# A two-layer diffusion backbone with sorted experts: the second mixer's norm by products with a diagonal, the larger experts from the fifth small one on, and the rows' gates formed ahead of the outputs

## The chip, the core and the metric

The kernel runs on one core of a Trainium2 chip. The metric is the device time of one execution in microseconds (us), in the median of several runs; less is better. A profile is one execution recorded by the hardware, and its span runs from the first instruction to the last.

The core has five engines with queues of their own, each of which works strictly in the order in which its instructions stand: TensorE (PE in the profile; PEld is its weight load), VectorE (DVE), ScalarE (ACT), GpSimd (POOL) and SyncE (SP), which here only issues transfers. An engine waits at an instruction until what it needs is there, and everything behind it in its queue waits as well.

## The reference, cut to what matters

Two layers over 512 latent tokens and 256 context tokens of width 1024, all in float32. Each layer has a mixer (attention) and a mixture of 32 experts of which each token uses two.

```python
for l in range(2):
    h_lat = modulate(x, norm_mix[l], sh1, sc1)      # rms_norm(x) * g * (1 + scale) + shift
    h_ctx = modulate(ctx, norm_mix[l], csh1, csc1)
    o_lat, o_ctx = mixer_ab(...) if l == 0 else mixer_c(...)
    x = x + gt1 * o_lat
    tokens = ...        # l == 0: context and latent tokens, 768; l == 1: latent ones, 512
    f = hier_moe(tokens, ...)                       # top 2 of 32 experts for each token
    x = x + gt2 * f                                 # l == 0: ctx = ctx + cgt2 * f[:, :c_len] too

def expert_block(xb, e):
    return (silu(xb @ w1[e]) * (xb @ w3[e])) @ w2[e]
```

An expert's output row is weighted by its token's router weight and by a gate row of 1024 numbers: gt2 for latent tokens, cgt2 for context tokens. In the second layer only latent tokens are left, so there is one gate row.

## The kernel before, in words

The program goes through setup, the first mixer with its output projection and router, the first expert stage (about 490 to 1030 us in the profile), the second mixer (mixer_c, 1030 to 1420), its output projection and router (to 1500), and the second expert stage (to the end).

*The expert stages* (moe). The experts are sorted by load while the program runs. Positions of the sorted list have a fixed room: two "static" ones and the NBIG[l] fullest ("big", 6 in the first stage and 3 in the second) hold 96 rows, the others ("small", 24 and 27) hold 64; what lies beyond goes through a loop (overflow) behind a branch, which had nothing to do in this execution. Each expert's weights come in six loads of 1 MB (line 1577) into a rotation of buffers. For each, GpSimd gathers token rows (line 1522), TensorE turns them (line 1600) and forms h = x w1 and x w3 (line 1619; 1625 for the 32 rows beyond 64 of a large expert), ScalarE and VectorE form silu and product (lines 1674, 1679), TensorE turns that (line 1688) and multiplies by w2 (tile py). VectorE then weighs py into a tile y (weigh, lines 1534 to 1538): in the first stage with sw[:, 0] times the context gate g[0] or sw[:, 1] times the latent gate g[1], one of the two weights being zero in each row, which takes three operations; in the second stage one operation is enough. GpSimd scatters y with addition into the token rows in memory (xd in the first stage, out_dram in the second, line 1528). A large expert has a second, smaller tile yt for its rows beyond 64 and so a second scatter. There are three buffers for y and one for yt.

The list `order` (lines 1540 to 1547) sets which expert is worked on when: the static ones, then the small ones with a large one behind every fourth (first stage) or ninth (second stage) of them, from the second small one on.

*What orders the instructions.* Both stages and the mixers are written as pieces (S.op) with an engine, an estimated duration, dependencies and buffer tokens (take, give). A list scheduler (Sched.run) plays these through with its own estimates before anything runs, and the order it finds is the order in which TensorE, VectorE, ScalarE and GpSimd get their instructions. SyncE's own order is made by the layer underneath.

*The second mixer's start* (mixer_c). Its six token tiles (oo[:, t]: two of context, four latent, 128 tokens each) are loaded from xd (line 1860). In memory order its buffers lie where the expert stage had its own, so its first ScalarE casts (wh, line 327) and its first loads (nw_q, nw_k, line 533) wait until the last scatter has landed. Function tokens (lines 1871 to 1881) then does for each tile: ScalarE sums the squares (line 1874), VectorE finds the reciprocal root in nine small steps (lines 289 to 301, tile css), ScalarE scales the tile in place by it, in two halves (line 1877), and flip_mod (lines 641 to 666) turns it. There TensorE transposes eight 128x128 blocks in two groups of four (line 649, tile ht), VectorE or ScalarE apply the modulation, a column scale and a shift, block by block (lines 660, 658), and the result is split into a high and a low part (chh, line 327; chl, line 330), which the projection's products (pp, lines 266 to 268) read. Context tiles are projected 256 columns wide and latent ones 384. Pieces of the projection need, beside the tiles, tables for the rotary embedding, which GpSimd forms (rope_tables, lines 528 to 548; it also issues the loads nw_q and nw_k).

Of the kernel before, what the change touches and what calls it, by code (L numbers as in the profile page):

```python
# [25 lines left out]
HD = 64  # L26
DE = 512
# [17 lines left out]
NY = 3  # L45
# [40 lines left out]
CMW = 2  # L86
# [154 lines left out]
class Backbone:  # L241
# [396 lines left out]
            self.nc.tensor.matmul(o, pts[:, b], v[b], start=b == 0, stop=b == len(v) - 1)  # L638


    def flip_mod(self, c, l, t, x, deps, tag, done, bufs, give=()):
        nc, S, v, s = self.nc, self.S, 0 if t >= NCT else 1, slice(t * 128, (t + 1) * 128)
        for g in range(2):
            cur = []

            def flip(g=g, cur=cur):
                cur.append(c.psm.tile([128, 4, 128], F32, tag="pt", name="ht"))
                for j in range(4):
                    nc.tensor.transpose(cur[0][:, j], x(4 * g + j), self.id)

            def affine(e, j, g=g, cur=cur):
                if len(cur) == 1:
                    cur.append(c.sb.tile([128, 768], F32, tag=tag, name="h", bufs=bufs)[:, 0:512]
                               .rearrange("p (j f) -> p j f", j=4))
                k = 4 * g + j
                ak, bk = self.a1[l][:, k, v:v + 1], self.mcol[l][:, k, v:v + 1]
                if e == "ACT":
                    nc.scalar.activation(cur[1][:, j], cur[0][:, j], AF.Identity, bias=bk, scale=ak)
                else:
                    nc.vector.tensor_scalar(cur[1][:, j], cur[0][:, j], ak, bk, op0=OP.mult, op1=OP.add)  # L660

            k = slice(4 * g, 4 * g + 4)
            a = S.op("PE", 0.43, flip, deps[g:g + 1] if l else deps, take=("pt", tag), give=give if g else ())
            js = [S.op(("DVE", "ACT"), (0.2, 0.25), lambda e, j=j, affine=affine: affine(e, j), [a]) for j in range(4)]
            a = S.op("-", 0.0, lambda: None, js, give=("pt",))
            done[t, g] = self.split_ops(lambda k=k, cur=cur: (c.hh[:, k, s], c.hl[:, k, s], cur[1]), 512, [a], give=(tag,))
# [823 lines left out]
    def moe(self, l, nt, oo):  # L1490
        nc, tc, i = self.nc, self.tc, self.i
        r, mm = self.rt, self.nc.tensor.matmul
        tok = nt * 128
        with ExitStack() as st:
            pool = lambda n, b, **k: st.enter_context(tc.tile_pool(name=n, bufs=b, side="right", **k))
            one = pool("moe1", 1)
            sb = pool("moesb", 2)
# [5 lines left out]
            gates, tails = [], []  # L1503
# [23 lines left out]
            def scatter(src, idx, n=DE):  # L1527
                nc.gpsimd.indirect_dma_start(out=rows(sums, n), out_offset=bass.IndirectOffsetOnAxis(ap=idx, axis=0),  # L1528
                                             in_=src, in_offset=None, bounds_check=tok * (D // n) - 1,
                                             oob_is_err=False, compute_op=OP.add)  # L1530


            def weigh(dst, src, sw, g):
                nc.vector.scalar_tensor_tensor(dst, src, sw[:, 0], g[0], op0=OP.mult, op1=OP.mult)  # L1534
                if l == 0:
                    t = sb.tile([128, DE], F32, tag="yc", name="yc", bufs=1)[:src.shape[0]]
                    nc.vector.scalar_tensor_tensor(t, src, sw[:, 1], g[1], op0=OP.mult, op1=OP.mult)
                    nc.vector.tensor_tensor(dst, dst, t, op=OP.add)  # L1538

            nb, early = NBIG[l], self.early  # L1540
            small, big = list(range(nb, NE - NST)), list(range(nb))
            order = [("static", e) for e in range(NST)]
            every = len(small) // nb
            for j, q in enumerate(small):
                order.append(("small", q))
                if j % every == 1 and big:
                    order.append(("big", big.pop(0)))
            slots = NW + self.npre + self.nmoe + NT // 2 + NEXT
            first = NW + self.npre + self.nmoe
# [2 lines left out]
            S = self.S = Sched((FPE, FDVE, FACT, FPOOL), (GPE, GDVE, GACT, GPOOL), wr=slots - len(early),  # L1552
                               xg=NX, xt=NXT, x=2, h=3, py=2, tr=3, g=2, y=NY, yt=1, u=1, v=1)
            W, X, last = {}, {}, {"mm": None, "second": None}
# [153 lines left out]
            def second(s, kind):  # L1708
                x, isb = X[s], kind != "small"
                for half in range(2):  # L1710
                    def mul(half=half):
                        if half == 0:
                            x["y"] = [pyp.tile([128, DE], F32, tag="py", name="py") for _ in range(2 if isb else 1)]
                        products(x["y"], lambda k: x["gt"][:, k, 0:CS], (lambda k: x["gt"][:, k, CS:]) if isb else None,
                                 (2 * half, 2 * half + 1), 4,
                                 lambda m, k: W[s, "w2", k // 2][0][:, 1024 * (k % 2) + 512 * m:1024 * (k % 2) + 512 * m + 512])

                    S.pos = 10.0 * s + 14.0
                    p = last["second"] = S.op("PE", 2.9 if isb else 1.9, mul, [W[s, "w2", half][1], x["gop"], last["second"]],
                                              take=() if half else ("py", "py") if isb else ("py",), give=("g",) if half else ())  # L1720
                    free(s, ("w2",), half, p)

                def out(g, token, src, gs, bufs):
                    x["o", g] = sb.tile([128, DE], F32, tag=token, name=token, bufs=bufs)[:x["parts"][g][0]]
                    weigh(x["o", g], src(), x["sw", g], gs)

                a = S.op("DVE", 0.8 if l else 2.2, lambda: out(0, "y", lambda: x["y"][0], gates, NY), [p], take=("y",), give=("py",))
                a = S.op("POOL", 1.05, lambda: scatter(x["o", 0], x["idx", 0]), [a])
                S.op("DMA", 1.1, lambda: None, [a], give=("y",))
                if isb:  # L1730
                    b, u = add_tails("py", lambda: x["y"][1], [p])
                    a = S.op("DVE", 0.8 if l else 2.2, lambda: out(1, "yt", u, tails, 1), [b], take=("yt",), give=("u",))
                    a = S.op("POOL", 1.05, lambda: scatter(x["o", 1], x["idx", 1]), [a])
                    S.op("DMA", 1.1, lambda: None, [a], give=("yt",))

# [89 lines left out]
    def mixer_c(self, oo):  # L1825
        nc, tc, i = self.nc, self.tc, self.i
        S = self.S = Sched((DPE, DDVE, DACT, DPOOL), (EPE, EDVE, EACT, EPOOL), wr=NW, pt=2, s=2, po=1, pp=1, p0=2, p1=2, pts=2, qdup=1, qhl=2, rt=1, rt1=1, hss=2, khl=1,
                           grp=2, vv=3, whl=5, mrow=2, mw=CMW)
        keep, st = ExitStack(), ExitStack()
        left = lambda n, b, **k: st.enter_context(tc.tile_pool(name=n, bufs=b, **k))  # L1830
        right = lambda n, b, **k: keep.enter_context(tc.tile_pool(name=n, bufs=b, side="right", **k))
        c = self.c = type("C", (), {})()
# [3 lines left out]
        big = left("cp", 1)  # L1836
# [21 lines left out]
        ld = S.op("DMA", 8.0, lambda: None)  # L1858

        sd = [S.op("DMA", 1.5, lambda t=t: nc.sync.dma_start(oo[:, t], self.source(1, t)), [ld]) for t in range(NT)]  # L1860
        ld = S.op("DMA", 1.0, loads, sd)
# [7 lines left out]
        hdone, spare = {}, []  # L1869

        def tokens(t):
            s = slice(t * 128, (t + 1) * 128)
            X, ss = oo[:, t], one.tile([128, 2], F32, name=f"css{t}")
            sq = S.op("ACT", 1.2, lambda: nc.scalar.activation(
                c.hh[:, :, s], X.rearrange("p (k f) -> p k f", k=KD), AF.Square, accum_out=ss[:, 0:1]), [sd[t]])
            r = self.rstd(lambda: (ss[:, 1:2], ss[:, 0:1]), D, [sq], once=t < ONCE)
            xs = [S.op("ACT", 0.6, lambda m=m: nc.scalar.activation(
                X[:, 512 * m:512 * m + 512], X[:, 512 * m:512 * m + 512], AF.Copy, scale=ss[:, 1:2]), [r]) for m in range(2)]
            self.flip_mod(c, 1, t, lambda k: X[:, 128 * k:128 * k + 128], xs, "p0", hdone, 2)
            if t >= 4:  # L1880
                spare.extend([hdone[t, 0], hdone[t, 1]])

        for t in range(NT):
            S.pos = -38.0 + t
            tokens(t)
        tables = S.op("POOL", 4.0, tables, [], pos=-24.0)


        def lam_dots():
# [3 lines left out]
        a = S.op("POOL", 0.5, lam_dots, [ld], pos=-20.0)  # L1893
        a = S.op("DVE", 0.2, lambda: nc.vector.tensor_reduce(ls, lp[:, 0::2], axis=AX.X, op=OP.add), [a], pos=-20.0)
        a = S.op("ACT", 0.1, lambda: nc.scalar.activation(ls, ls, AF.Exp), [a], pos=-20.0)
# [14 lines left out]
        room = [oo[:, 4 + m // 2, 512 * (m % 2):512 * (m % 2) + 512] for m in range(4)]  # L1910
# [169 lines left out]
```

## Time and profile before

| | us |
|---|---|
| runs | 2027.43, 2023.10, 2027.01 |
| median | 2027.01 |
| the profiled execution | 2027.06 |
| its span | 2025.2 |
| TensorE busy in the span | 1767.7 (87%) |
| VectorE busy | 1022.0 (50%) |
| ScalarE busy | 559.3 (28%) |
| GpSimd busy | 335.7 (17%) |

The views used here are these. The windows give each engine's busy time in a stretch of the span, the clock granted to TensorE (1.00 is full speed) and the mean share of time in which the 16 DMA engines were busy; this share comes out a little above 1 when they are full. The timeline lists instructions in order of time: start, duration, engine, line, operation, output<-input, count, and in brackets the idle time of the engine just before it and what ended that, as far as the semaphore events tell. The grouped lines give for each line and shape the busy time, the mean duration in ns, and the idle time before. For TensorE the duration of one instruction includes its way through the array, and neighbours overlap; start to start tells the rate. Indirect DMAs on GpSimd show the time in which it prepares them, not their landing.

### The profile page before, as it was taken

What the parts mean: (1) busy time and instruction counts of PE and PEld (TensorE: products, weight loads), DVE (VectorE), ACT (ScalarE), POOL (GpSimd) and SP (SyncE); (2) the same over time, 40 slices, a digit from 0 to 9 for tenths busy, and PEclk for the clock granted to TensorE, in tenths of its full rate; (3) what the DMA queues carried; (4) which work ended last, traced back from release to release, by engine and by line L of the source; (5) the groups of instructions that cost most, each with busy time, mean ns of one, the idle gap of its engine ahead of it and who ended that gap; (6) DMA issues with size and microseconds to landing.
All of it is one profiled execution on the core that took longest, in us unless ns stands there. A gap on an engine that the chain in (4) does not pass through costs nothing. (4 is left out here: it accounts for less than half of the span.)

```text
span 2025.2 us, 27795 instructions
## 1 busy us (share of the span) xinstructions
PE 1767.7 (87%) x10130; PEld 1013.8 (50%) x10130; DVE 1022.0 (50%) x2628; ACT 559.3 (28%) x1278; POOL 335.7 (17%) x365
## 2 busy tenths in 40 slices
PE   4999998896999898888938999998869998978986
PEld 2798776684233222222327989996752332222322
DVE  3788878597333232333357788887872211211211
ACT  4565556321110000000044555555311100000000
POOL 1001000012122112111112232221021221111111
PEclk8999999897999999999959999999879999999999
DMA  8502314337999999999933222115569999999996
GB/s 354 188 20 82 141 47 167 146 125 262 356 385 403 407 407 410 407 405 406 389 121 115 74 74 63 32 42 183 206 241 343 386 408 413 409 413 413 409 412 249
DMA packets 98782, 532.42 MB, mean 263 GB/s; under 512 B 22840, under 2 KB 23208, under 8 KB 43344
## 3 DMA queue, kind: packets, MB, share of 16 engines
q1 hardware_dynamic: 82544, 509.53, 63.4%
q0 software_dynamic: 16096, 21.05, 4.4%
q8 instruction: 82, 1.34, 0.3%
q14 instruction: 60, 0.49, 0.1%
HBM read 517.45 MB, written 29.03 MB: 270 GB/s over the span
## 5 line engine op out<-in xcount | busy, mean ns | idle before, releaser
L1619 PE MATMUL h<-wr,x 128*64 128x512 f32 x2000 | 530.3, 612 | 92.1 <-DMA wr<-in_w_dram 90.0
L1619 PEld LDWEIGHTS h<-wr,x 128*64 128x64 f32 x2000 | 149.4, 138 | 401.8 <-issue 225.4
L1605 DVE COPY x<-trx 128x512 f32<-128x512 f32 (+1 forms) x67 | 43.8, 659 | 462.3 <-PE trx L1600 462.2
L1619 PE MATMUL py<-wr,gt 128*64 128x512 f32 x1024 | 240.4, 599 | 2.3 <-DMA wr<-in_w_dram 1.7
L1674 ACT ACTIVATE sl<-h 64x512 f32<-64x512 f32 x64 | 37.8, 591 | 702.7 <-PE h L1619 696.0
L1619 PEld LDWEIGHTS py<-wr,gt 128*64 128x64 f32 x1024 | 68.5, 136 | 137.5 <-issue 121.8
L266 PE MATMUL pp<-wh,chh 128*128 128x384 f32 (+1 forms) x384 | 132.6, 345 | 4.5 <-ACT vv L692 2.7
L1679 DVE TENSOR_TENSOR gp<-sl,h 64x512 f32<-64x512 f32 x64 | 68.0, 1062 | 122.4 <-ACT sl L1674 121.8
L268 PE MATMUL pp<-wh,chl 128*128 128x384 f32 (+1 forms) x384 | 124.6, 325 | 1.1 <-DVE chl L330 1.1
L267 PE MATMUL pp<-wl,chh 128*128 128x384 f32 (+1 forms) x384 | 124.6, 325 | 0.0
L1522 POOL DMA_INDIRECT xg<-h2d,ridx x64 | 68.3, 1067 | 281.3 <-PE trx L1600 242.8
L1534 DVE SCALAR_TENSOR_TENSOR y<-py,rsw,g 128x512 f32<-128x512 f32 x64 | 48.1, 751 | 126.4 <-PE py L1619 124.7
L623 PE MATMUL ptp<-cst,p 128*128 128x128 f32 x592 | 95.4, 284 | 17.6 <-DVE p L1955 4.5
L1528 POOL DMA_INDIRECT xd<-y,ridx x32 | 53.5, 1672 | 234.2 <-DVE y L1538 146.1
L1528 POOL DMA_INDIRECT out_dram<-y,ridx x32 | 52.7, 1646 | 216.0 <-DVE y L1534 177.3
L623 PEld LDWEIGHTS ptp<-cst,p 128*128 128x128 f32 x592 | 69.0, 143 | 36.5 <-issue 15.1
L1193 POOL TENSOR_TENSOR h2p<-xi,bc 128x512 f32<-128x512 f32 x10 | 16.2, 1618 | 410.7 <-DVE xi L1190 320.8
L946 ACT ACTIVATE p<-s,nbias,r 128x256 f32<-128x256 f32 (+3 forms) x96 | 76.6, 801 | 17.9 <-DVE nbias L940 8.0
L266 PEld LDWEIGHTS pp<-wh,chh 128*128 128x128 f32 x384 | 74.7, 195 | 11.4 <-ACT vv L692 7.4
L627 ACT COPY pts<-ptp 128x384 f32<-128x384 f32 (+2 forms) x114 | 54.9, 488 | 77.9 <-PE ptp L623 77.4
L268 PEld LDWEIGHTS pp<-wh,chl 128*128 128x128 f32 x384 | 74.3, 193 | 1.4 <-DVE chl L330 1.4
L267 PEld LDWEIGHTS pp<-wl,chh 128*128 128x128 f32 x384 | 74.7, 194 | 0.0
(347 smaller groups left out, 3262.3 us busy)
## 6 DMA issues: line engine op xcount, KB each, us to landing
wr<-in_w_dram SPq DMA_DIRECT2D x378, 1024.0 KB
wr<-in_w_mod_dram SPq DMA_DIRECT2D x48, 1024.0 KB
wr<-in_wc_dram SPq DMA_DIRECT2D x16, 768.0 KB
wr<-in_wab_dram SPq DMA_DIRECT2D x8, 768.0 KB
oo<-in_w_dram SPq DMA_DIRECT2D x6, 1024.0 KB
h2d<-h2p SPq DMA_DIRECT2D x10, 512.0 KB
bc<-modrow SPq DMA_DIRECT2D x9, 512.0 KB
wr<-in_w_out_ab_dram SPq DMA_DIRECT2D x4, 1024.0 KB
```

Of the source, the lines that this page charges most:

```text
L266: mm(ps, xh, wh, start=start, stop=False)
L267: mm(ps, xh, wl, start=False, stop=False)
L268: mm(ps, xl, wh, start=False, stop=stop)
L623: nc.tensor.transpose(st[g][:, b], st["p"][:, (g + b) * 128:(g + b + 1) * 128], self.id)
L627: f(st["pts"][:, g:g + n], st[g][:, :n])
L946: nc.scalar.activation(p[:, a:b], st["s"][:, a:b], AF.Exp, bias=nb()[:, m:m + 1], scale=hr()[:, m:m + 1], accum_out=z["ssum"][:, h + m:h + ...
L1522: nc.gpsimd.indirect_dma_start(out=dst, out_offset=None, in_=rows(self.h2d[l], n), in_offset=bass.IndirectOffsetOnAxis(ap=idx, axis=0), bo ...
L1528: nc.gpsimd.indirect_dma_start(out=rows(sums, n), out_offset=bass.IndirectOffsetOnAxis(ap=idx, axis=0), in_=src, in_offset=None, bounds_ch ...
L1534: nc.vector.scalar_tensor_tensor(dst, src, sw[:, 0], g[0], op0=OP.mult, op1=OP.mult)
L1605: (nc.scalar.copy if e == "ACT" else nc.vector.tensor_copy)(x["x"][:, 512 * g:512 * g + 4 * w].rearrange("p (k t) -> p k t", k=4), x["tr", g])
L1619: mm(out[0][CS * m:CS * m + CS], at(k), w(m, k), start=k == 0, stop=k == n - 1, tile_position=(0, CS * m), skip_group_check=True)
L1679: nc.vector.tensor_tensor(x["p"][dst].rearrange("t (k p) -> t p k", k=4), v(a), v(b), op=OP.mult)
```

## The change

There are three parts, and what follows from them in the order of instructions.

1. In the second mixer, the tile is no longer scaled in place. VectorE writes a 128x128 diagonal dg, the identity times the reciprocal root of each token, and flip_mod multiplies each block by it (an ordinary product where a transpose with the identity stood), so that turning and scaling are one. The diagonals lie in two buffers that later pieces use (qdup and csq), taken in turn. The tables of the rotary embedding now depend on the loads of the token tiles having been issued (`[ld]`).

2. In the expert stages, the first large expert comes behind the fifth small one, and the others behind every third (first stage) or seventh (second stage) from there.

3. In the first stage, the tile y is filled ahead of the output with the gates: sw[:, 0] * g[0] + sw[:, 1] * g[1], two operations that need the expert's gt but not its last product; then one multiplication by py is left (out). In the second stage only the buffer is taken sooner.

```diff
-    def flip_mod(self, c, l, t, x, deps, tag, done, bufs, give=()):
+    def flip_mod(self, c, l, t, x, deps, tag, done, bufs, give=(), by=None):
...
-                    nc.tensor.transpose(cur[0][:, j], x(4 * g + j), self.id)
+                    if by is None:
+                        nc.tensor.transpose(cur[0][:, j], x(4 * g + j), self.id)
+                    else:
+                        nc.tensor.matmul(cur[0][:, j], x(4 * g + j), by(), start=True, stop=True)
...
             def weigh(dst, src, sw, g):
...
+                if l:
+                    nc.vector.scalar_tensor_tensor(dst, src, sw[:, 0], g[0], op0=OP.mult, op1=OP.mult)
+                else:
+                    row_gates(dst, sw, g)
+                    nc.vector.tensor_tensor(dst, src, dst, op=OP.mult)
+            def row_gates(dst, sw, g):
+                nc.vector.tensor_scalar(dst, g[0], sw[:, 0], None, op0=OP.mult)
+                nc.vector.scalar_tensor_tensor(dst, g[1], sw[:, 1], dst, op0=OP.mult, op1=OP.add)
...
-            every = len(small) // nb
+            every = (len(small) - 4) // nb
             for j, q in enumerate(small):
                 order.append(("small", q))
-                if j % every == 1 and big:
+                if j >= 4 and (j - 4) % every == 0 and big:
                     order.append(("big", big.pop(0)))
...
-                a = S.op("DVE", 0.8 if l else 2.2, lambda: out(0, "y", lambda: x["y"][0], gates, NY), [p], take=("y",), give=("py",))
+                a = S.op("DVE", 0.02 if l else 1.1, lambda: room(0, "y", gates, NY), [x["gop"]], take=("y",))
+                a = S.op("DVE", 0.8, lambda: out(0, lambda: x["y"][0], gates), [p, a], give=("py",))
...
-            xs = [S.op("ACT", 0.6, lambda m=m: nc.scalar.activation(
-                X[:, 512 * m:512 * m + 512], X[:, 512 * m:512 * m + 512], AF.Copy, scale=ss[:, 1:2]), [r]) for m in range(2)]
-            self.flip_mod(c, 1, t, lambda k: X[:, 128 * k:128 * k + 128], xs, "p0", hdone, 2)
+            def diagonal():
...
+                nc.vector.tensor_scalar(dg[0], self.id, ss[:, 1:2], None, op0=OP.mult)
+            r = S.op("DVE", 0.2, diagonal, [r], take=(room,))
+            self.flip_mod(c, 1, t, lambda k: X[:, 128 * k:128 * k + 128], [r, r], "p0", hdone, 2, give=(room,), by=lambda: dg[0])
...
-        tables = S.op("POOL", 4.0, tables, [], pos=-24.0)
+        tables = S.op("POOL", 4.0, tables, [ld], pos=-24.0)
```

The lines are renumbered by the change (line 1528 before is 1531 after, 1860 is 1877, 649 is 652).

GpSimd's queue at the end of the first expert stage, before: scatters of y and yt into xd, and the gathers xg that stand between them; the branch to the overflow follows.

```order
L1528 DMA xd<-y,ridx_3696 1536x512
L1522 DMA xg_5678<-h2d_89,ridx_3696 128x512
L1528 DMA xd<-y,ridx_3696 1536x512 x4
L1528 DMA xd<-yt,ridxt 1536x512
L1528 DMA xd<-y,ridx_3696 1536x512 x2
```

And the same place after the change:

```order
L1531 DMA xd<-y,ridx_3696 1536x512
L1525 DMA xg_5678<-h2d_89,ridx_3696 128x512
L1531 DMA xd<-y,ridx_3696 1536x512 x2
L1531 DMA xd<-yt,ridxt 1536x512
L1531 DMA xd<-y,ridx_3696 1536x512 x4
```

The scatter yt of the last large expert has moved from third to fifth from the end.

SyncE's queue where the second mixer begins, before: the rows' weights nw, the six tiles oo, the small vector lp, and two loads of weights (wr).

```order
L533 DMA nw_q<-in_qn_c_dram 128x64
L533 DMA nw_k<-in_kn_c_dram 128x64
L1860 DMA oo<-xd 128x1024 x6
L1852 DMA lp<-in_lam_c_dram 128x256
L1758 DMA wr<-in_wc_dram 128x1536
L381 DMA wr<-in_w_mod_dram 128x2048
```

And after the change:

```order
L1877 DMA oo<-xd 128x1024 x6
L1869 DMA lp<-in_lam_c_dram 128x256
L533 DMA nw_q<-in_qn_c_dram 128x64
L533 DMA nw_k<-in_kn_c_dram 128x64
L381 DMA wr<-in_w_mod_dram 128x2048 x2
```

The nw loads have moved behind the tiles. The last load of wc stands ahead of the branch to the overflow now, together with the three others, and a load of w_mod that stood among them has moved behind nw_k.

TensorE's queue in the second mixer, where the turning of the last tiles meets the projection of the first latent tile (products of width 384), before:

```order
L268 MATMUL pp<-wh,chl 128x256
L649 MATMUL ht<-cst,oo 128x128 x16
L266 MATMUL pp<-wh,chh 128x384
L267 MATMUL pp<-wl,chh 128x384
L268 MATMUL pp<-wh,chl 128x384
```

And after, from the fourth tile's second half on:

```order
L268 MATMUL pp<-wh,chl 128x256
L652 MATMUL ht<-dg,oo 128x128 x4
L266 MATMUL pp<-wh,chh 128x384
L267 MATMUL pp<-wl,chh 128x384
L268 MATMUL pp<-wh,chl 128x384
```

Where all sixteen blocks of the last two tiles stood ahead of the first product of width 384, only the last four of the fourth tile do now; the last two tiles' blocks follow in fours, with six to twelve products between them. On ScalarE the twelve scalings are gone from this place, and the sums of squares of the last three tiles stand together.

More of the change, by code (lines that the diff above doesn't have):

```diff
@@ L1533, in weigh @@
             def weigh(dst, src, sw, g):
[L1534 to L1538, printed above, removed]
+                if l:
[6 more added lines that the diff above has]
+                nc.vector.scalar_tensor_tensor(dst, g[1], sw[:, 1], dst, op0=OP.mult, op1=OP.add)
             nb, early = NBIG[l], self.early
@@ L1721, in second, with room, out @@
                     free(s, ("w2",), half, p)
-                def out(g, token, src, gs, bufs):
+                def room(g, token, gs, bufs):
                     x["o", g] = sb.tile([128, DE], F32, tag=token, name=token, bufs=bufs)[:x["parts"][g][0]]
-                    weigh(x["o", g], src(), x["sw", g], gs)
-                a = S.op("DVE", 0.8 if l else 2.2, lambda: out(0, "y", lambda: x["y"][0], gates, NY), [p], take=("y",), give=("py",))
+                    if l == 0:
+                        row_gates(x["o", g], x["sw", g], gs)
+                def out(g, src, gs):
+                    if l:
+                        weigh(x["o", g], src(), x["sw", g], gs)
+                    else:
+                        nc.vector.tensor_tensor(x["o", g], src(), x["o", g], op=OP.mult)
+                a = S.op("DVE", 0.02 if l else 1.1, lambda: room(0, "y", gates, NY), [x["gop"]], take=("y",))
+                a = S.op("DVE", 0.8, lambda: out(0, lambda: x["y"][0], gates), [p, a], give=("py",))
                 a = S.op("POOL", 1.05, lambda: scatter(x["o", 0], x["idx", 0]), [a])
@@ L1731, in second @@
                     b, u = add_tails("py", lambda: x["y"][1], [p])
-                    a = S.op("DVE", 0.8 if l else 2.2, lambda: out(1, "yt", u, tails, 1), [b], take=("yt",), give=("u",))
+                    a = S.op("DVE", 0.02 if l else 1.1, lambda: room(1, "yt", tails, 1), [x["gop"]], take=("yt",))
+                    a = S.op("DVE", 0.8, lambda: out(1, u, tails), [b, a], give=("u",))
                     a = S.op("POOL", 1.05, lambda: scatter(x["o", 1], x["idx", 1]), [a])
@@ L1827, in mixer_c @@
         S = self.S = Sched((DPE, DDVE, DACT, DPOOL), (EPE, EDVE, EACT, EPOOL), wr=NW, pt=2, s=2, po=1, pp=1, p0=2, p1=2, pts=2, qdup=1, qhl=2, rt=1, rt1=1, hss=2, khl=1,
-                           grp=2, vv=3, whl=5, mrow=2, mw=CMW)
+                           grp=2, vv=3, whl=5, mrow=2, mw=CMW, csq=1)
         keep, st = ExitStack(), ExitStack()
@@ L1876, in tokens @@
             r = self.rstd(lambda: (ss[:, 1:2], ss[:, 0:1]), D, [sq], once=t < ONCE)
-            xs = [S.op("ACT", 0.6, lambda m=m: nc.scalar.activation(
-                X[:, 512 * m:512 * m + 512], X[:, 512 * m:512 * m + 512], AF.Copy, scale=ss[:, 1:2]), [r]) for m in range(2)]
-            self.flip_mod(c, 1, t, lambda k: X[:, 128 * k:128 * k + 128], xs, "p0", hdone, 2)
+            dg, room = [], "qdup" if t % 2 else "csq"
+            def diagonal():
+                dg.append(c.sb.tile([128, 2, 2, HD], F32, tag="qdup", name="dg", bufs=1).rearrange("p a b d -> p (a b d)")[:, 0:128] if t % 2
+                          else c.sb.tile([128, 128], F32, tag="csq", name="dg", bufs=1))
+                nc.vector.tensor_scalar(dg[0], self.id, ss[:, 1:2], None, op0=OP.mult)
+            r = S.op("DVE", 0.2, diagonal, [r], take=(room,))
+            self.flip_mod(c, 1, t, lambda k: X[:, 128 * k:128 * k + 128], [r, r], "p0", hdone, 2, give=(room,), by=lambda: dg[0])
             if t >= 4:
```

## The prediction

> **What bounds the kernel now.** I read the windows first, to see which engine sets the pace in each stage, then TensorE's waits, then the timeline of the seam between the first expert stage and the second mixer, instruction by instruction. The windows give for each stretch the busy time (and count) of TensorE, its weight loads, VectorE, ScalarE and GpSimd, then TensorE's granted clock, the DMA share and GB/s.
>
> ```profile
> 600.00:700.00 100.00, 92.26 (x438) 29.06 (x436) 33.73 (x47) 7.52 (x14) 22.86 (x17) 1.00 1.02 404
> 1010.00:1020.00 10.00, 5.02 (x22) 1.20 (x18) 4.20 (x6) 0.00 (x0) 1.56 (x1) 0.91 0.40 138
> 1020.00:1030.00 10.00, 0.00 (x0) 0.00 (x0) 0.00 (x0) 0.00 (x0) 1.56 (x1) 0.50 0.11 16
> 1570.00:1580.00 10.00, 10.00 (x52) 3.60 (x50) 3.18 (x5) 0.59 (x1) 5.47 (x4) 1.00 0.95 344
> 1580.00:1590.00 10.00, 10.00 (x62) 2.73 (x58) 1.44 (x2) 0.37 (x1) 2.66 (x2) 1.00 0.98 376
> 1800.00:1900.00 100.00, 83.92 (x384) 26.70 (x382) 17.08 (x21) 7.48 (x15) 15.90 (x12) 1.00 1.02 413
> ```
>
> Inside both expert stages the DMA share stands at 1.02 and TensorE waits for weights, so the order of the experts can't shorten the stream itself, except where the share is below that. Between 1020 and 1030 us nothing computes at all. The timeline of that hole:
>
> ```profile
> 998.72 1.56 POOL L1528 DMA_INDIRECT xd<-y,ridx  x1 [11.69 <-DVE y L1538]
> 1008.37 1.42 POOL L1528 DMA_INDIRECT xd<-yt,ridxt  x1 [8.09 <-DVE gp L1679]
> 1009.21 1.94 PE L1619 MATMUL py<-wr,gt 128*64 128x512 f32 x8 [0.55 <-DMA wr<-in_w_dram]
> 1012.63 0.69 DVE L1538 TENSOR_TENSOR y<-y,yc 128x512 f32<-128x512 f32 x1
> 1014.18 1.94 PE L1619 MATMUL py<-wr,gt 128*64 128x512 f32 x8 [0.46 <-DMA wr<-in_w_dram]
> 1015.69 1.56 POOL L1528 DMA_INDIRECT xd<-y,ridx  x1 [5.90 <-issue]
> 1017.61 0.69 DVE L1538 TENSOR_TENSOR y<-y,yc 128x512 f32<-128x512 f32 x1
> 1023.74 1.56 POOL L1528 DMA_INDIRECT xd<-y,ridx  x1 [6.48 <-SPq L1772]
> 1030.11 0.34 SPq L533 DMA_DIRECT2D nw_q<-in_qn_c_dram  x1
> 1030.50 0.42 SPq L533 DMA_DIRECT2D nw_k<-in_kn_c_dram  x1
> 1030.51 3.03 ACT L327 CAST wh<-wr 128x768 fp32r<-128x768 f32 x4 [23.45 <-DMA xd<-y,ridx]
> 1031.05 3.51 SPq L1860 DMA_DIRECT2D oo<-xd  x6
> 1035.89 1.06 ACT L1874 ACTIVATE chh<-oo 128x1024 fp32r<-128x1024 f32 x1 [2.35 <-DMA oo<-xd]
> ```
>
> The last output is ready at 1018.30 (1017.61 + 0.69), but its scatter starts at 1023.74. The four scatters start 9.65, 7.32 and 8.05 us apart: each adds into the same tensor xd and starts only when the one ahead has landed. The reasons in the brackets (a branch, "issue") are guesses of the view; the even spacing, with the data long ready, is what I go by. The chain holds four links because the last large expert, with two scatters, stands third from the end. At 1030.11 the last one has landed, and ScalarE and the DMA queue both come free on it: that seam is what the change can move.
>
> **The change part by part.** Everything is counted against the profiled execution, 2027.06 us (its span is 2025.2), which is the median, 2027.01, to 0.05 us.
>
> *Experts in another order, first stage.* The last large one now has four small ones behind it, 24 loads of 1 MB or about 60 us of stream at 404 GB/s, so its scatters are done long before. Left of the chain are the last two small outputs. *Gates formed ahead:* behind the last product stands one VectorE operation instead of three. The one before last ends its products at 1011.15 (1009.21 + 1.94); one operation of 0.69 makes 1011.9, and the queue's step, 0.28 elsewhere at a scatter that waited for data alone (its y done at 984.65, start 984.93), 1012.2. The rows for this and for the next part, timeline first, then loads with their sizes:
>
> ```profile
> 983.96 0.69 DVE L1538 TENSOR_TENSOR y<-y,yc 128x512 f32<-128x512 f32 x1
> 984.93 2.11 POOL L1528 DMA_INDIRECT xd<-y,ridx  x1 [15.90 <-DVE y L1538]
> 2009.53 1.56 POOL L1528 DMA_INDIRECT out_dram<-y,ridx  x1 [13.00 <-DVE y L1534]
> 2014.47 1.56 POOL L1528 DMA_INDIRECT out_dram<-y,ridx  x1 [3.39 <-DVEq L1772]
> ...
> 1072.78 0.73 POOL L555 TENSOR_TENSOR qk<-qk,nw_k 128x256 f32<-128x256 f32 x1 [27.58 <-ACT sq L701]
> ...
> wr<-in_w_dram SPq DMA_DIRECT2D x378, 1024.0 KB
> oo<-xd SPq DMA_DIRECT2D x6, 512.0 KB
> ```
>
> The last scatter follows one interval later. I take 8.05, that of the same pair before, so 1020.2; its landing took 6.37 (1030.11 - 1023.74), so 1026.6: 3.5 us earlier. Bounds of the interval: 9.65, the longest of the chain above (gain 1.9), and 4.94, the pair at the end of the second stage, where little else moved (then the last output's own time decides, 1016.12 + 0.69 + 0.28 + 6.37 = 1023.5, gain 6.6). The end of the weight stream, which both rely on, I leave where it is, as the same bytes are loaded. The added gate operations lie beside other work: VectorE is busy 33.73 of 100 us there. If that cover failed, two operations of 0.7 us would stand before a product of an early expert, where TensorE is full.
>
> *SyncE's queue.* The two nw loads no longer stand ahead of the six oo loads: 0.94 us (1031.05 - 1030.11) is taken off their issue; at least 0.5, should the first issue after the wait cost more. The nw loads now land behind 3 MB of oo and GpSimd forms its tables later. The cover is long: the first operation on them is at 1072.78, after a wait of 27.58 us, and those tables were done when it began. What the queue gains in addition, the second half of the next group's weights ahead of the branch, nobody waits for.
>
> *The mixer's norm.* Twelve ScalarE scalings go, six small VectorE operations that form a diagonal come, and the eight transposes of a token become products with it.
>
> ```profile
> L1877 ACT ACTIVATE oo<-oo,css 128x512 f32<-128x512 f32 x12 | 8.3, 715 | 0.8 <-DVE css L301 0.5 <-DVE rsv L289 0.3
> L660 DVE TENSOR_SCALAR h<-ht,a,mcol 128x128 f32<-128x128 f32 x36 | 12.9, 406 | 6.6 <-ACT h L658 4.7 <-PE ht L649 1.9
> L289 DVE TENSOR_SCALAR rsv<-css 128x1 f32<-128x1 f32 x6 | 0.9, 148 | 2.1 <-ACT chh L1874 2.1
> 1307.10 0.96 PE L623 MATMUL ptp<-cst,p 128*128 128x128 f32 x6 [0.66 <-DVE p L1955]
> 1307.82 0.36 PE L266 MATMUL pp<-wh,chh 128*128 128x256 f32 x1
> 1309.31 1.50 PE L638 MATMUL po<-vv,pts 128*128 128x128 f32 x12
> 1310.65 0.60 PE L729 MATMUL ptk<-cst,khl 128*128 128x128 f32 x4
> 1036.00:1071.30 35.30, 18.40 (x97) 16.61 (x97) 25.40 (x97) 26.68 (x51) 3.95 (x10) 0.65 0.32 118
> 1040.50:1071.30 30.80, 18.40 (x97) 16.61 (x97) 22.38 (x84) 22.68 (x44) 0.69 (x2) 0.67 0.21 74
> 1059.02 1.97 PE L649 MATMUL ht<-cst,oo 128*128 128x128 f32 x8 [4.90 <-ACT oo L1877]
> 1070.53 1.11 PE L649 MATMUL ht<-cst,oo 128*128 128x128 f32 x4 [1.82 <-ACT oo L1877]
> 1071.30 0.67 PE L266 MATMUL pp<-wh,chh 128*128 128x384 f32 x1
> ```
>
> The trace has real products of this very shape: twelve (L638) take 1.34 us to the next instruction, 0.11 each, and six transposes (L623) 0.72, or 0.12 each. So I cost the products at nothing. A page speaks against that: the Trainium skill, "TensorE: Matmul & The Clock Gate", section "Terms", says that transpose mode is four times faster for FP32. Read as a price for the plain product, it gives the third rival below; these rows don't bear it out.
>
> A diagonal (128x128, from SBUF) has no row; it lies between 0.15 (one column, L289) and 0.41 (same size, from PSUM), and I take 0.3, in the middle. The first token's first scaling of 0.72 becomes that: 0.4 us. Behind it, from 1040.5 to 1071.3, TensorE is idle for 12.4 of 30.8 us, on chains through ScalarE and VectorE. 6.72 us of it (4.90 + 1.82) end on a scaling. Not all goes, since the sums of squares and the root ahead of it take their time too; but the new order also lets products of width 384 begin before the last transposes, where now all wait until 1071.30. I take two thirds, 4.5 us. The floor is 0, if the planner's new order gives it back; the ceiling is VectorE's own work: 25.40 busy of 35.30, plus 6 x 0.3, leaves 8.1. Behind this ramp the instructions stand as before, so what is gained is kept.
>
> *Second stage's order.* There the share is 0.95 and 0.98 while the first large expert fills TensorE (1570 to 1590); a small one in its place frees buffers sooner. 0.7 + 0.4 us to reach 1.02 make 1.1 at most, 0 at least; I take 0.8. In the first stage the same place shows no loss.
>
> Sum: 3.5 + 0.9 + 0.4 + 4.5 + 0.8 = 10.1, so 2027.06 - 10.1 = 2017.0. All upper ends give 6.6 + 0.9 + 0.6 + 8.1 + 1.1 = 17.3 (2009.8), all lower ends 1.9 + 0.5 + 0.3 = 2.7 (2024.4).
>
> **The rivals.** *The ramp gives nothing:* with ScalarE relieved, VectorE's in-order queue (22.38 of 30.8 us busy, now with six operations more) is late next, and TensorE waits for its splits instead. For it: 36 affine operations of 0.41 are VectorE's already. Against: ScalarE was as busy, and is what the two longest waits name. It leaves 5.6 us: 2021.5. *The chain isn't shortened:* the interval of the last pair is set by transfers still queued (the share is 0.40 until 1020), not by the scatter, and stretches to 9.65; with a ramp of nothing that is the lower end, 2024.4, within 0.2%. For it: those queued loads stay. *The product costs four times a transpose* (slower): 3 x 0.12 us at full clock, twice that at the 0.50 that the clock has behind the hole, for 48 of them is 17 to 35 us of TensorE, say 26; 12.4 idle us swallow part, the other terms give 5.2 back: 2027.06 + 26 - 12.4 - 5.2 = 2035. It decides from an extra of (12.4 + 5.2) / 48 = 0.37 us each. Against it stand the L638 rows.
>
> **How the numbers follow.** Forecast 0.62, ramp of nothing 0.20, chain not shortened 0.12, dear products 0.06. 2017.0 is the first case; the range 2009.8 to 2024.4 takes in the first three, with all bounds. No change that can be told is within 0.2%, 4.1 us, so down to 2023.0. The first case and nearly all of the second lie below that: faster 0.80; the third and what is left of the second: same 0.14; slower 0.06.
>
> **What would show it.** The seam: two scatters a chain apart at the end, the last output's behind one VectorE operation, ScalarE's idle stretch of 23.45 us cut by 3 to 4, oo issued first. The ramp: no wait on a scaling, the first product of width 384 some 5 us sooner after the first sum of squares than the 35.4 us (1071.30 - 1035.89) of now. The second stage: share 1.02 from 1570 on. Wrong it would be if the last two scatters still stand four deep, if the products take more than 0.2 us each at full clock, or if the ramp is as long as before with VectorE named.

## The result, and the profile after

The changed kernel takes 2013.12 us in the median of five runs (2011.08 to 2016.79), the kernel before 2027.01 in five beside them (2023.10 to 2030.90): the ratio is 0.9938, with a 95% interval of 0.9923 to 0.9953, or 13.9 us between the medians where 10.0 were forecast. The profiled execution took 2011.99 us with a span of 2010.2, against 2025.2: 15.0 us between the spans.

The windows after the change, with the same columns as before (the last three are TensorE's granted clock, the DMA share and GB/s):

```profile
1010.00:1020.00 10.00, 5.95 (x28) 1.84 (x24) 2.52 (x4) 0.37 (x1) 1.56 (x1) 1.00 0.42 150
1020.00:1030.00 10.00, 0.00 (x0) 0.00 (x0) 1.52 (x2) 2.38 (x4) 1.56 (x1) 0.57 0.33 100
1036.00:1071.30 35.30, 28.15 (x188) 26.83 (x188) 27.35 (x100) 22.76 (x51) 8.90 (x17) 0.92 0.17 69
```

The hole behind the stage is still there. In the ramp, the stretch that held 18.40 us of TensorE's work now holds 28.15; the ramp begins some 5 us sooner in it. The timeline of the seam after the change:

```profile
1011.72 0.69 DVE L1740 TENSOR_TENSOR y<-py,y 128x512 f32<-128x512 f32 x1 [1.76 <-PE py L1627]
1012.53 3.98 PE L1627 MATMUL py<-wr,gt 128*64 128x512 f32 x16 [0.46 <-ACT gt L1700]
1012.68 1.56 POOL L1531 DMA_INDIRECT xd<-y,ridx  x1 [13.38 <-DVE y L1740]
1016.56 0.69 DVE L1740 TENSOR_TENSOR y<-py,y 128x512 f32<-128x512 f32 x1 [2.97 <-PE py L1627]
1020.98 1.56 POOL L1531 DMA_INDIRECT xd<-y,ridx  x1 [6.73 <-DMA xd<-y,ridx]
1026.58 2.81 SPq L1877 DMA_DIRECT2D oo<-xd  x6
1030.83 0.33 SPq L533 DMA_DIRECT2D nw_q<-in_qn_c_dram  x1
1030.94 1.06 ACT L1891 ACTIVATE chh<-oo 128x1024 fp32r<-128x1024 f32 x1 [0.29 <-DMA oo<-xd]
1034.03 0.29 DVE L1900 TENSOR_SCALAR dg<-cst,css 128x128 f32<-128x128 f32 x1
1034.53 3.75 PE L652 MATMUL ht<-dg,oo 128*128 128x128 f32 x16 [18.02 <-ACT chh L1891]
```

Two scatters stand a chain apart, the last output (ready at 1017.25) behind one operation of VectorE, and oo ahead of nw. The last row is the surprise: one token's eight products are sixteen instructions.

Six distances place the gain of the profiled executions, 15.0 us in all. They run between the starts of rows as above; the first scores are the first product s<-kt, and the order of these products on TensorE is the same in both:

| us | before | after | gain |
|---|---|---|---|
| last scatter starts | 1023.74 | 1020.98 | 2.76 |
| from there to the first sum of squares | 12.15 | 9.96 | 2.19 |
| from there to the first scores | 69.04 | 62.56 | 6.48 |
| from there to the output projection's first product | 324.99 | 323.53 | 1.46 |
| from there to the loads of the second stage's gates | 70.18 | 68.68 | 1.50 |
| from there to the end | 525.1 | 524.5 | 0.6 |

The last three rows, 3.6 us, differ as much between kernels that are the same there, so they are not put down to the change; the figures stand further below.

### The profile page after: what moved, and what is told of

Same layout as the page of the kernel before. It is cut to its first block, busy times and chain, and to the rows that moved or that the text cites. A ratio compares the mean times of both kernels' runs of the same rounds, so it can differ in the third digit from the quotient of the medians.

```text
span 2010.2 us, 27841 instructions
## 1 busy us (share of the span) xinstructions
PE 1768.0 (88%) x10178; PEld 1015.5 (51%) x10178; DVE 1010.9 (50%) x2625; ACT 553.4 (28%) x1275; POOL 336.4 (17%) x365
## 5 line engine op out<-in xcount | busy, mean ns | idle before, releaser
L1613 DVE COPY x<-trx 128x512 f32<-128x512 f32 (+1 forms) x75 | 48.1, 651 | 485.9 <-PE trx L1608 485.8
L931 DVE TENSOR_REDUCE nbias<-s 128x1 f32<-128x768 f32 (+3 forms) x80 | 64.8, 814 | 19.2 <-PE s L609 16.9
```

The lines of the kernel that those rows point to most:

```text
L931: nc.vector.tensor_reduce(nb(), st["s"][:, off:off + w].rearrange("p (n f) -> p n f", n=n), axis=AX.X, op=OP.max, negate=True)
L1613: (nc.scalar.copy if e == "ACT" else nc.vector.tensor_copy)(x["x"][:, 512 * g:512 * g + 4 * w].rearrange("p (k t) -> p k t", k=4), x["tr", g])
```

## The experiments

Twelve kernels, each timed in five rounds against the kernel before. The two distances are those of the table's second and third rows; nw or oo names what stands first in SyncE's queue.

| kernel | median us | ratio to before, 95% | scatter to squares | squares to scores |
|---|---|---|---|---|
| order_only | 2022.79 | 0.9975 to 0.9993 | 13.23, nw | 68.55 |
| gates_only | 2032.56 | 1.0022 to 1.0046 | 12.81, nw | 67.48 |
| order_gates | 2024.82 | 0.9984 to 1.0004 | 12.63, nw | 67.57 |
| gates_yt2 | 2025.14 | 0.9986 to 1.0003 | 13.16, nw | 68.41 |
| tables_late_before | 2023.20 | 0.9978 to 0.9998 | 9.81, oo | 68.30 |
| norm_only | 2017.31 | 0.9944 to 0.9971 | 9.73, oo | 62.29 |
| tables_early | 2018.78 | 0.9958 to 0.9980 | 13.39, nw | 65.13 |
| transposes_back | 2011.97 | 0.9916 to 0.9943 | 10.03, oo | 60.55 |
| mask_transpose | 2015.08 | 0.9924 to 0.9950 | 9.99, oo | 60.96 |
| warm | 2014.43 | 0.9925 to 0.9948 | 10.03, oo | 62.85 |
| warm_before | 2025.47 | 0.9989 to 1.0006 | 13.85, nw | 67.80 |
| warm_stages | 2013.61 | 0.9930 to 0.9957 | 10.02, oo | 62.48 |

The theory was the prediction's three parts, with the clock as what made the ramp gain more; its rivals were that one part carries all, and that the clock is a bystander.

**The three parts alone.**

```diff
 # order_only: before, with
+            every = (len(small) - 4) // nb
+                if j >= 4 and (j - 4) % every == 0 and big:
```

> The kernel before with the new order of the experts alone, in both stages. Theory (chain of scatters): the last two scatters of the first stage are those of two small experts, the one before last waits for its output's two operations more than in the changed kernel (about 1.4 us), the last follows an interval of 8 us later; so the mixer's loads are issued about 2 us sooner than the 1031.05 of before, and the second stage gives 0.7 to 0.9: 2.0 to 4.0 us faster than before in all. Rival (the stream sets the end, the order is worth nothing): within 1 us of before. Second rival (the order alone carries the whole seam, the gates nothing): 3.5 us or more at the seam.

It gained 3.7 us (medians of 2026.53 and 2022.79), as the theory had it. Its timeline, TensorE's last products of the stage and the last three scatters:

```profile
1015.49 1.94 PE L1619 MATMUL py<-wr,gt 128*64 128x512 f32 x8 [0.25 <-DMA wr<-in_w_dram]
1000.47 1.56 POOL L1528 DMA_INDIRECT xd<-y,ridx  x1 [12.57 <-DVE y L1538]
1014.92 1.56 POOL L1528 DMA_INDIRECT xd<-y,ridx  x1 [12.89 <-DVE y L1538]
1023.47 1.56 POOL L1528 DMA_INDIRECT xd<-y,ridx  x1 [6.99 <-DMA xd<-y,ridx]
```

The last scatter starts only 0.27 us sooner than before (1023.47 against 1023.74), but this execution's whole first stage lies later: the first load of its gates is issued at 487.76 instead of 485.50, ahead of anything that the edit touches. Counted from the end of TensorE's last product (1017.43 here, 1016.12 before), the last scatter starts 6.04 us behind it instead of 7.62. So the order alone does shorten the chain, to two links and by 1.6 us. This distance is 7.0 to 7.6 in the four profiles that leave this stage as before, 6.7 and 6.5 in the two with the gates alone (gates_only, gates_yt2, below), and 4.5 to 4.9 in the seven with both. The 0.7 to 0.9 us that were expected of the second stage aren't there (525.2 us from its gates' loads to the end, against 525.1); what else makes up the 3.7 is not shown.

```diff
 # gates_only: before, with row_gates, room and out of the change
+                a = S.op("DVE", 0.02 if l else 1.1, lambda: room(0, "y", gates, NY), [x["gop"]], take=("y",))
```

> The kernel before with the rows' gates formed ahead of the outputs alone. Theory (chain of scatters): the chain of four stands, but its first link waits for an output that is ready about 1.4 us sooner, so the seam comes 0 to 1.4 us sooner and the total is within 1.5 us of before. Rival (what stands behind the last product decides, not the chain): the mixer's loads are issued 1.4 us or more sooner and the last two scatters no longer wait for each other.

Both expectations fell: it is 6 us slower than before (2032.56 against 2026.53). The timelines of VectorE and TensorE at the front of the first stage, in this kernel:

```profile
558.13 0.48 DVE L1542 TENSOR_SCALAR yt<-g2t,rswt 64x512 f32<-64x512 f32 x1 [10.92 <-DMA xd<-yt,ridxt]
559.42 1.03 DVE L1684 TENSOR_TENSOR gp<-sl,h 64x512 f32<-64x512 f32 x1
560.50 0.69 PE L1693 MATMUL trg<-cst,gp 64*128 64x64 f32 x4 [4.85 <-DVE gp L1684]
```

The gates of the next large expert's yt stand in VectorE's queue until the last scatter of yt, of which there is one buffer, has landed. Behind them stands gp, for which TensorE waits 4.85 us. In the changed kernel VectorE waits at the same kind of place:

```profile
557.82 0.48 DVE L1545 TENSOR_SCALAR yt<-g2t,rswt 64x512 f32<-64x512 f32 x1 [6.63 <-DMA xd<-yt,ridxt]
```

What stands behind it there is wanted later: TensorE's wait for gp between 520 and 620 us (in total, times, longest) comes to

```profile
PE trg L1696 <- DVE gp L1687: 0.2, 1, 0.2
```

```diff
 # norm_only: before, with the diagonal, flip_mod(by=) and
+        tables = S.op("POOL", 4.0, tables, [ld], pos=-24.0)
```

> The kernel before with the mixer's norm by products with a diagonal alone (GpSimd's tables behind the loads of the tokens with it). Theory (scalings gone, then the clock comes back sooner): TensorE's clock is at half for under 10 us between the first products of the ramp and its end, against 25 us before; the ramp is 6 to 8 us shorter, the queue gives 0.9: 8 to 11 us faster than before. Rival (the ramp's gain needs the shorter hole of the seam, by where the clock's windows fall): 3 to 6 us faster. Second rival (SyncE's queue and the scalings alone, as the prediction had it): 5.8 us.

It gained 9.2 us, the ramp 6.75 (69.04 to 62.29), within the theory's numbers. Whether the clock was the reason is tested below.

**Order and gates together, and the cause of the loss.**

```diff
 # order_gates: before, with both of the parts above
 # gates_yt2: gates_only, with
-                               xg=NX, xt=NXT, x=2, h=3, py=2, tr=3, g=2, y=NY, yt=1, u=1, v=1)
+                               xg=NX, xt=NXT, x=2, h=3, py=2, tr=3, g=2, y=NY, yt=2, u=1, v=1)
+                    a = S.op("DVE", 0.02 if l else 1.1, lambda: room(1, "yt", tails, 2), [x["gop"]], take=("yt",))
```

> The kernel before with the experts' order and the gates ahead together, the mixer as before. Theory (the two need each other: the order takes the third user of the yt buffer away from the front, the gates take two operations out of the last chain): the last scatter starts near 1021 as in the changed kernel, the front of the stage loses nothing, the rest behind the last scatter is as before; 3 to 5 us faster than before, about 2022. Rival (the parts add up: 3.7 us gained by the order alone, 6 lost by the gates alone): 2 to 3 us slower than before.

> The kernel with the gates alone, and two buffers for the output yt of the large experts instead of one. Theory (with one buffer the gates of the next large expert wait in VectorE's queue for the scatter of the last, 10.9 us, and hold up what TensorE needs): that wait is under 2 us, TensorE does not stand at the front of the stage, and the loss of 6 us is gone: 2024.5 to 2027.5. Rival (the gate operations themselves, ahead of work that TensorE waits for, cost the time): still 2030 or more.

With a second buffer the loss is gone (2025.14), and no wait for yt stands among VectorE's waits from 520 to 1020: the cause is shown. Order and gates together gain 2.0 us of medians, below the 3 to 5 expected and above the sum of the two, which would be 2.3 slower; the interval takes in both no gain and the lower end of the theory. The last scatter, at 1020.86, is where it was expected.

**SyncE's queue.**

```diff
 # tables_early: the changed kernel, with
+        tables = S.op("POOL", 4.0, tables, [], pos=-24.0)
 # tables_late_before: before, with
+        tables = S.op("POOL", 4.0, tables, [ld], pos=-24.0)
```

> The changed kernel with GpSimd's tables free of the wait for the tokens' loads, as before, so that the two loads of nw stand ahead of the six of oo in SyncE's queue again. Theory (SyncE's queue): oo is issued 0.9 us later behind the last scatter's landing, and the whole is 0.5 to 1 us slower than the changed kernel. Rival (GpSimd's tables, 9 us later in the changed kernel, cost the mixer something): 0.5 us or more faster than the changed kernel.

> The kernel before with nothing but GpSimd's tables behind the tokens' loads, so that the six loads of oo go ahead of the two of nw. Theory (SyncE's queue: in the runs so far the first sum of squares starts 12.2 to 13.9 us behind the last scatter's start with nw first, 9.7 to 10.0 with oo first): 9.7 to 10.0 us here too, the total 2 to 3.5 us faster than before, about 2024. Rival (the queue is worth 0.9 us, and what the changed kernel with the tables early lost came from its own order of work in the ramp): within 1.5 us of before.

The queue is worth more than 0.9 us. By medians, nw first costs the changed kernel 5.7 (2018.78 against 2013.12), and oo first gains the one before 3.6 (2023.20 against 2026.83; that interval by itself, 0.4 to 4.5, would allow the 0.9). The distance from scatter to squares is the clearer measure. The timeline with nw first, in tables_early:

```profile
1020.25 1.56 POOL L1531 DMA_INDIRECT xd<-y,ridx  x1 [6.74 <-DMA xd<-y,ridx]
1026.51 0.34 SPq L533 DMA_DIRECT2D nw_q<-in_qn_c_dram  x1
1026.90 0.74 SPq L533 DMA_DIRECT2D nw_k<-in_kn_c_dram  x1
1027.76 3.25 SPq L1877 DMA_DIRECT2D oo<-xd  x6
1033.64 1.06 ACT L1891 ACTIVATE chh<-oo 128x1024 fp32r<-128x1024 f32 x1 [3.70 <-DMA oo<-xd]
```

And with oo first, in tables_late_before:

```profile
1025.20 1.56 POOL L1528 DMA_INDIRECT xd<-y,ridx  x1 [6.29 <-SPq L1772]
1030.71 3.04 SPq L1860 DMA_DIRECT2D oo<-xd  x6
1035.01 1.06 ACT L1874 ACTIVATE chh<-oo 128x1024 fp32r<-128x1024 f32 x1 [0.23 <-DMA oo<-xd]
```

Three things add up. The first load is issued 6.26 us behind the scatter when it is nw, 5.51 when it is oo; the two nw take 1.25 more; and the squares of oo's first tile start 5.88 us behind its issue instead of 4.30. Why the first issue and the tile come later behind nw, no run shows. In all seven profiles with oo first the squares start 9.7 to 10.0 us behind the scatter, in the seven with nw first 12.2 to 13.9 (the 13.9 is warm_before, below, whose first issue comes only 8.07 us behind the scatter; without it, 12.2 to 13.4). The rest of the loss in tables_early is in the ramp. There the planner puts an operation of the mixer's lambda elsewhere, and the table that ScalarE loads for it with it:

```profile
1057.65 1.28 ACT L1919 ACT_TABLE_LOAD   x1
```

In the changed kernel this stands at 1059.50, 28.6 us behind the first sum of squares instead of 24.0, and among modulations too. The ramp of tables_early is 2.57 us longer (65.13 against 62.56); whether the table load's place makes any of that wasn't tried.

**The product's price.**

```diff
 # transposes_back: the changed kernel, with
+                    if True:
+                        nc.tensor.transpose(cur[0][:, j], x(4 * g + j), self.id)
 # mask_transpose: the changed kernel, with
+                        nc.tensor.transpose(cur[0][:, j], x(4 * g + j), by())
+                nc.vector.tensor_scalar(dg[0], self.id, ss[:, 1:2], 0.0, op0=OP.mult, op1=OP.is_gt)
```

> The changed kernel with the 48 products with the diagonal turned back into transposes of the unscaled tokens; the diagonal is formed and waited for as before, but the norm's scaling is left out of what is computed. Theory (a product costs about 0.2 us at full clock, a transpose 0.12): 48 x 0.08 to 0.1 is 4 to 5 us of TensorE, of which the idle time of the ramp hides about half: 1.5 to 4 us faster than the changed kernel. Rival (product and transpose cost the same, as the prediction had it): within 0.5 us of the changed kernel. Second rival (four times a transpose): 10 us or more faster.

> The changed kernel with the 48 products turned into transposes that still wait for the same operation of VectorE: it forms a matrix of zeros and ones from the same column instead of the diagonal, so every wait and every engine's order stays; the norm's scaling is left out of what is computed. Theory (a product takes about 0.2 us at full clock and 0.47 at half, a transpose 0.12 and 0.25): the first eight take 1.8 us less at half clock, ahead of everything, and the rest 0.08 each, of which waiting hides half: 2 to 4 us faster than the changed kernel, about 2010. Rival (product and transpose cost the same): within 0.5 us of the changed kernel, about 2013.

The first was badly made: an unscaled transpose needs no diagonal, so the first ones ran at 1031.67, ahead of the squares at 1032.03, and the wait was gone as well. The second keeps every wait and order. TensorE's groups of these instructions (busy us, mean ns), first in the changed kernel, then in mask_transpose:

```profile
L652 PE MATMUL ht<-dg,oo 128*128 128x128 f32 x96 | 15.0, 313 | 19.4 <-ACT chh L1891 18.0 <-DVE dg L1900 1.4
```

```profile
L652 PE MATMUL ht<-dg,oo 128*128 128x128 f32 x48 | 9.3, 338 | 19.2 <-ACT chh L1891 18.1 <-DVE dg L1900 0.7 <-ACT h L661 0.4
```

A plain product of this shape is two instructions (96 for 48 products), and the 48 cost 5.7 us more of TensorE in all, 0.12 each at the clocks that the two ramps have. The ramp was 1.6 us shorter with transposes (60.96 against 62.56); in the medians (2015.08 and 2013.12) nothing of it shows.

**The clock.**

```diff
 # warm: the changed kernel (warm_before: the one before), ahead of the mixer's pieces
+        wm = psm.tile([128, 4, 128], F32, tag="pt", name="wm")
+        for k in range(80):
+            nc.tensor.matmul(wm[:, k % 4], self.id, self.id, start=True, stop=True)
 # warm_stages: the changed kernel, 15 such products ahead of each stage's S.run()
```

> The changed kernel with 80 products of the 128x128 identity with itself on TensorE in the hole between the first expert stage and the mixer (about 16 us at full clock, from 1016.5 on; their result goes nowhere). Theory (the clock falls behind the hole and is half the ramp's cost that is left): the clock is at 1.0 when the ramp begins, the first eight products take 1.8 us instead of 3.75, the half-speed windows of the ramp go, 2 to 4 us faster than the changed kernel, about 2010. Rival (the ramp is a chain through ScalarE and VectorE, TensorE's speed in it is idle time): within 1 us of the changed kernel.

> The kernel before with the same 80 products in its hole (from 1016 on, done by about 1033 of the hole that ends at 1040.5). Theory (the clock, once it has fallen, comes back only with a nearly full window, and the waits for scalings keep it from that): the windows at half speed behind the hole, 25 us of them before, are halved at least, and the ramp is 3 to 6 us shorter than in the kernel before, about 2021 to 2024. Rival (the waits for scalings by themselves cost the time, the clock is a bystander): within 1.5 us of before, with the waits for scalings as long as before or longer.

> The changed kernel with 15 products of the identity with itself on TensorE at the front of each expert stage (about 1497.5 to 1504.5 in the second, while it waits for the first tokens). Theory (the clock is at 0.5 for 30.7 us at the front of each stage, and TensorE is full behind it for 80 us with the weights' stream below its 1.02): the clock is at 1.0 some 13 us sooner, TensorE does 5 to 7 us of work sooner in each stage, and 2 to 6 us of each are kept: 2002 to 2009. Rival (the stream of weights binds the stages anyway, as the ramp was bound by its chain when the clock was held up there): within 1.5 us of the changed kernel.

The windows of warm show how far the clock was held:

```profile
1020.00:1030.00 10.00, 10.00 (x92) 10.00 (x91) 0.97 (x2) 1.83 (x3) 1.56 (x1) 1.00 0.29 74
1030.00:1040.00 10.00, 8.34 (x75) 8.14 (x73) 6.57 (x23) 6.16 (x12) 0.00 (x0) 1.00 0.86 332
1040.00:1050.00 10.00, 7.75 (x40) 7.25 (x40) 9.01 (x33) 5.46 (x12) 6.35 (x13) 0.66 0.38 161
```

It was at 1.00 through the hole and the first token's products, and fell again behind them: 0.66 from 1040 to 1050, where the changed kernel has this:

```profile
1040.00:1050.00 10.00, 7.18 (x46) 6.78 (x46) 9.32 (x35) 5.32 (x11) 6.34 (x13) 0.83 0.35 148
```

Nothing came of it: the scores follow the squares by 62.85 us (62.56 without), although the first token's products took 1.95 us instead of 3.75. The extra products also ended late and put the first real one at 1036.39, 4.87 behind the squares instead of 3.59, which takes back 1.28 of these 1.80 us. In warm_before the distance fell by 1.2 (69.04 to 67.80) and the total is not to be told from before; there too the clock fell again, to 0.57 from 1040 to 1050.

So the gains that the theory of the clock expected, 2 to 4 and 3 to 6 us, did not come, and a full clock in the hole and at the first products is worth nothing that can be told. No run held the clock through the whole ramp, though. In the kernel before it is at 0.67 from 1050 to 1060, 0.84 to 1070 and 0.69 to 1080; in the changed one it is at 1.00 from 1050 on. How much of the ramp's gain is this return, how much the scalings' steps that are gone, and how much the new order of products, is not separated. That the steps on ScalarE and VectorE carry it is the likelier reading, not a shown one.

In warm_stages the clock returned sooner too, 0.85 against the changed kernel's 0.50 from 500 to 510:

```profile
500.00:510.00 10.00, 7.36 (x49) 5.98 (x50) 2.85 (x10) 0.00 (x0) 6.04 (x7) 0.85 1.01 409
```

Its last scatter of the first stage starts 2.9 us sooner than the changed kernel's (1018.09), but the total, 2013.61, can't be told from that kernel's. No version here beats that one by what can be told.

## Why the prediction was right, point by point

*Seam, 3.5 forecast.* The mechanism was right: the last scatter started at 1020.98 (forecast 1020.2), 8.30 us behind the one ahead (8.05 taken), 2.76 sooner than before. It starts 4.47 us behind the end of TensorE's last product (1016.51) instead of 7.62. The mixer's first load came at 1026.58, where 1026.6 was forecast, and that is luck: the scatter was 0.8 later than forecast, and the load followed it by 5.60 instead of the 6.37 that were taken, as in all runs with oo first (5.5 to 5.7). As a part of the total, order and gates with the second stage are worth 2.0 us on the kernel before and 4.2 on norm_only (2017.31 to 2013.12), against 3.5 + 0.8; the intervals of the latter two kernels overlap, so the 4.2 is rough.

*The cover of the gates.* The step that named VectorE's idle time as cover failed. Their own time is covered; what was left out is that they take their buffer sooner, and so wait for a scatter in an in-order queue. Alone that costs 6 us. With the new order VectorE still waits, but TensorE doesn't.

*SyncE's queue, 0.9 forecast.* The most mis-sized term: by distances 2.2 us up to the squares (before against after) to 3.4 (tables_early against after), and by medians 3.6 on the kernel before; the 5.7 of tables_early has the longer ramp in it. The step counted the two issues alone; that the first issue starts later when it is nw, and that the first squares then follow oo's issue later, was not costed.

*First scaling 0.4, ramp 4.5.* The squares-to-scores distance fell by 6.48. The norm without the queue's part is worth 5.9 (norm_only against tables_late_before) or 6.0 (tables_early against order_gates), so the 4.9 was 1 us short. The diagonal costs 0.29 as taken, and no wait names a scaling any more. The first product of width 384 came 26.3 us behind the first squares (1057.22) instead of 35.4: 9.1 sooner where the forecast's sign was 5, of which the scores keep 6.48. Of the rivals, the ramp of nothing is refuted, and of the chain not shortened the stretched interval, 9.65, which measured 8.30.

*Products at nothing.* The step is wrong in its reading: x12 in the L638 row counts instructions, of which a product takes two, so a product was 0.22 there and not 0.11. In the changed kernel four of them (eight instructions) take 0.81 us to the next instruction at a clock of 1.00 (1051.04 to 1051.85), 0.20 each, and the 80 of warm took 18.10, 0.23 each: the sign of being wrong, more than 0.2 at full clock, was all but met. The price is about twice a transpose, not four times, as the rival had it from the Trainium skill, "TensorE: Matmul & The Clock Gate", section "Terms". Of the 5.7 us that this makes, the ramp was 1.6 longer; the rest went into TensorE's idle time. That the sum survived a wrong price is luck.

*Second stage, 0.8.* Not shown. From its gates' loads to the end 0.6 us were gained, but this distance is 522.9 to 525.1 us in the six profiles with the old order and 524.1 to 526.4 in the seven with the new one (523.1 in warm_stages, with its extra products): the new order is not faster there by what can be told. The share reached 1.01 from 1570 as forecast, but it was 0.86 between 1550 and 1560.

*Behind the second mixer's ramp*, where the prediction held gains to be kept, 3.0 us more appeared (1.46 and 1.50) though the order there is the same. From the first scores to the output projection the fourteen profiles take 322.9 to 325.0 us, and the kernel before is among the longest; for the 1.50 see the last section.

*The sum.* By medians, the queue gave 3.6 where 0.9 was forecast, the norm 5.9 where it was 4.9, and order, gates and second stage 2.0 where it was 4.3: 11.5 in all, 10.1 forecast, 13.9 measured. That the misses go both ways is luck; the 2.4 us that are left lie within what the intervals, 2 to 3 us to either side, leave open.

## What to carry to other kernels

Before an operation is moved ahead, ask what its buffer waits for and who stands behind it in that in-order queue: an operation of 0.5 us held VectorE for 10.9. When the order of loads behind a wait changes, cost the landing of what follows too, and not only the issues. A count in a profile's row is one of instructions: divide by what one product really issues before taking a price from it. And compare starts with a landmark of the same execution: the 1.6 us that the order alone takes off the chain hid behind a stage that lay 2.26 us later as a whole.

## What was not expected of the hardware

The same instructions took 68.7, 70.2 or 71.6 us from the output projection's first product to the second stage's gates, and in the fourteen profiles nothing between these (three, nine and two of them). The windows of just this stretch, before, after, and in norm_only:

```profile
1429.92:1500.10 70.18, 63.88 (x355) 52.68 (x355) 57.59 (x207) 15.24 (x39) 6.82 (x5) 0.95 0.56 210
```

```profile
1417.03:1485.71 68.68, 62.39 (x355) 51.74 (x355) 57.40 (x207) 15.22 (x39) 6.54 (x4) 0.98 0.57 217
```

```profile
1420.94:1492.57 71.63, 65.33 (x355) 53.66 (x355) 57.79 (x207) 15.22 (x39) 6.85 (x5) 0.93 0.54 206
```

There are 355 TensorE instructions in each, and the granted clock of 0.98, 0.95 and 0.93 goes with the time. The Trainium skill, "TensorE: Matmul & The Clock Gate", section "Part 1: The HAM clock gate (the "warmup" mystery)", says that the clock follows a window that runs free of the kernel. Steps of 1.5 us are not at odds with it, but no run here moved that window by itself. So a step of 1.5 us in such a stretch is not put down to an edit.
